# Transposing bf16 pairs as 32-bit words and using all 128 matmul columns for one matrix, in a batched matmul on one core

## The chip, the cores and the metric

One core of a Trainium2 chip. The metric is device time in microseconds (us), as the median of several executions of the same kernel.

## The reference

```python
# x [8, 16, 256, 512] fp32, weight [8, 16, 512, 384] fp32 -> out [8, 16, 256, 384] fp32
def reference(x, weight):
    return np.matmul(x, weight).astype(np.float32)
```

There are 128 independent products of a 256 x 512 matrix with a 512 x 384 matrix. Inputs and outputs together are 167.77 + 50.33 = 218.1 MB.

## The kernel before

The kernel goes through the batches two at a time ("a pair"). For a pair it loads 1 MB of x and two weights of 768 KB, casts both to bf16 on VectorE, transposes x on TensorE (16 tiles of 128 x 128), copies the transposed tiles from PSUM (the buffer into which TensorE's results go) on VectorE, multiplies, evacuates the products on ScalarE and stores 768 KB. All loads and stores are issued by SyncE.

```python
groups = [2] * ((B - GX) // 2) + [1] * GX     # GX = 2: 63 pairs, then two single batches
LAG = 4                                        # a store is issued four pairs late
...
def transpose_x(x_sb, RG):
    ...
    for r0 in range(0, R, 4):
        nc.vector.tensor_copy(out=x_bf[:, r0 : r0 + 4], in_=x_sb[:, r0 : r0 + 4])   # fp32 -> bf16
        for r in range(r0, r0 + 4, 2):
            pt = psum_t.tile([P, 2, KO, P], bf16, name="pt")
            for rr in range(2):
                for ko in range(KO):
                    nc.tensor.transpose(pt[:, rr, ko, :], x_bf[:, r + rr, ko::KO], identity)
            j = r % RG
            nc.vector.tensor_copy(out=x_t[:, j : j + 2, :, :, r // RG], in_=pt[:])
...
for n, G in enumerate(groups):
    ...                                        # C = 128 // G rows of each batch, RG row groups
    x_sb = load_x(b); w_sb = [load_w(b + i) for i in range(G)]
    x_t = transpose_x(x_sb, RG)
    w_bf = [...]                               # both weights cast to bf16
    if last:
        while waiting: store(nc.sync)
    for r in range(0, RG, 2):
        po = psum_o.tile([P, 2, 512], fp32, name="po")
        for rr in range(2):
            for ko in range(KO):
                for i in range(G):             # two batches side by side, 64 columns each
                    c0 = (b % GX + i) * CX
                    nc.tensor.matmul(po[i * C : (i + 1) * C, rr, :N],
                                     x_t[:, r + rr, ko, c0 : c0 + CX, :], w_bf[i][:, ko, :],
                                     start=(ko == 0), stop=(ko == KO - 1))
        nc.scalar.copy(out=out_sb[:, r : r + 2, :], in_=po[:, :, :N])
    waiting.append(...)
    if len(waiting) > LAG or last: store(nc.sync)
```

## Time and profile before

| | before |
|---|---|
| time, median of 3 executions | 526.35 us (526.27 to 526.38) |
| span of the profiled execution | 524.1 us |
| busiest compute engine | TensorE, 65% |
| DMA rate from 5 to 510 us | 423 GB/s |
| a pair of batches | 8.03 us |

The prediction below shows the lines that say what bounds this kernel. Four groups of instructions are what the change is about. A line names the source line, engine, operation, what is written and read with shapes, and the count; after the bar stand the total busy time in us and the mean duration of one in ns; after the second bar the idle time ahead of them and what ended most of it.

```profile
L125 PE MATMUL po<-w_bf,x_t 128*64 128x384 bf16 (+1 forms) x2032 | 271.0, 400 | 136.3 <-DVE w_bf L110 135.9
...
L132 ACT COPY out_sb<-po 128x768 f32<-128x768 f32 x128 | 102.5, 801 | 416.0 <-PE po L125 404.5
...
L86 DVE COPY x_t<-pt 128x1024 bf16<-128x1024 bf16 x128 | 83.6, 696 | 59.2 <-PE pt L82 59.2
L82 PE MATMUL pt<-identity,x_bf 128*128 128x128 bf16 x1024 | 70.3, 222 | 44.1 <-DVE x_bf L77 43.7
```

There are 2,032 matmuls of mostly 64 columns, 1,024 transposes, and 128 evacuating copies of all 128 partitions. ScalarE stands idle for 416 us; it has room for twice as many copies.

### The profile page before, as it was taken

The numbers are of one execution on the slowest core, as the hardware profiler recorded it, in microseconds if no ns is written. First come the engines' busy times: TensorE is split into PE (matmuls) and PEld (weight loads), VectorE is DVE, ScalarE is ACT, GpSimd is POOL, SyncE is SP. The second block draws the span as 40 slices with busy tenths as digits, with TensorE's granted clock in tenths as the row PEclk, the third lists the DMA queues.
The fourth block names the chain that finished last, engine by engine and source line by source line (L and its number), as shares of the span: only waits on it lengthen the run. The fifth ranks groups of instructions, "written<-read, shape, count | busy, mean of one in ns | idle before, by whom it ended". The sixth has DMA issues, their size and how long they took to land.

```text
span 524.1 us, 7422 instructions
## 1 busy us (share of the span) xinstructions
PE 339.3 (65%) x3056; PEld 231.8 (44%) x3056; DVE 273.4 (52%) x320; ACT 103.8 (20%) x129; POOL 0.7 (0%) x6
## 2 busy tenths in 40 slices
PE   4666758558576665675857657567666586556664
PEld 2444435345444443443534435444344354344442
DVE  4565464564554645546456455564554645645543
ACT  0222122121121121212212112212121121121221
POOL 0000000000000000000000000000000000000000
PEclk9989797986978889979798887988788879898888
DMA  8999999999999999999999999999999999999996
GB/s 347 418 413 423 422 424 420 424 424 419 426 420 423 423 419 425 422 424 422 424 424 423 421 425 423 425 422 423 425 423 424 423 424 425 423 422 425 423 425 272
DMA packets 37041, 218.59 MB, mean 417 GB/s; under 512 B 4112, under 2 KB 4112, under 8 KB 28816
## 3 DMA queue, kind: packets, MB, share of 16 engines
q1 hardware_dynamic: 37008, 218.12, 99.9%
q8 instruction: 24, 0.39, 0.3%
q14 instruction: 9, 0.07, 0.0%
HBM read 167.77 MB, written 50.33 MB: 416 GB/s over the span
## 4 chain that ended last, share of the span: by engine, by line
DMA 97%; PE 1%; DVE 1%; issue 0%; ACT 0%; SPq 0%; ACTq 0%; DVEq 0%
DMA x_sb<-in_x_dram 94%; DMA w_sb<-in_weight_dram 3%; PE po L125 1%; DVE x_t L86 0%; DVE x_bf L77 0%; DVE w_bf L110 0%; ACT out_sb L132 0%; PE pt L82 0%; SPq L60 0%; ACTq L132 0%; DVEq L77 0%
## 5 line engine op out<-in xcount | busy, mean ns | idle before, releaser
L125 PE MATMUL po<-w_bf,x_t 128*64 128x384 bf16 (+1 forms) x2032 | 271.0, 400 | 136.3 <-DVE w_bf L110 135.9
L125 PEld LDWEIGHTS <-x_t 128*64 128x64 bf16 (+1 forms) x2032 | 171.5, 132 | 219.8 <-DVE w_bf L110 122.8
L132 ACT COPY out_sb<-po 128x768 f32<-128x768 f32 x128 | 102.5, 801 | 416.0 <-PE po L125 404.5
L77 DVE CAST x_bf<-x_sb 128x2048 bf16<-128x2048 f32 x64 | 78.5, 1227 | 182.0 <-DMA x_sb<-in_x_dram 182.0
L110 DVE CAST w_bf<-w_sb 128x1536 bf16<-128x1536 f32 x128 | 116.7, 952 | 1.9 <-DMA w_sb<-in_weight_dram 1.9
L86 DVE COPY x_t<-pt 128x1024 bf16<-128x1024 bf16 x128 | 83.6, 696 | 59.2 <-PE pt L82 59.2
L82 PE MATMUL pt<-identity,x_bf 128*128 128x128 bf16 x1024 | 70.3, 222 | 44.1 <-DVE x_bf L77 43.7
L82 PEld LDWEIGHTS <-x_bf 128*128 128x128 bf16 x1024 | 60.3, 115 | 67.7 <-DVE x_bf L77 63.5
L132 ACT ACT_TABLE_LOAD x1 | 1.3, 1283 | 0.7 <-PEq L156 0.7
masks.py:199 POOL TENSOR_SCALAR_AFFINE_SELECT identity<-identity 128x128 bf16<-128x128 bf16 x1 | 0.3, 294 | 0.1
masks.py:197 POOL MEMSET identity<- 128x128 bf16 x1 | 0.2, 205 | 0.3 <-POOLq L156 0.3
L156 POOL MEMSET const-bfloat16-1.0<- 128x1 bf16 x1 | 0.1, 102 | 0.0
L156 POOL MEMSET const-uint8-127<- 128x1 uint8 x1 | 0.1, 102 | 0.0
L156 POOL MEMSET const-float32-0.0<- 128x1 f32 x1 | 0.1, 99 | 0.2 <-issue 0.2
L156 POOL MEMSET const-float32-1.0<- 128x1 f32 x1 | 0.1, 99 | 0.0
## 6 DMA issues: line engine op xcount, KB each, us to landing
w_sb<-in_weight_dram SPq DMA_DIRECT2D x128, 768.0 KB, 16.0
x_sb<-in_x_dram SPq DMA_DIRECT2D x64, 1024.0 KB, 16.0
out_dram<-out_sb SPq DMA_DIRECT2D x63, 768.0 KB, 16.0
out_dram<-out_sb SPq DMA_DIRECT2D x2, 384.0 KB, 3.0
```

The source lines that it names most:

```text
L77: nc.vector.tensor_copy(out=x_bf[:, r0 : r0 + 4], in_=x_sb[:, r0 : r0 + 4])
L82: nc.tensor.transpose(pt[:, rr, ko, :], x_bf[:, r + rr, ko::KO], identity)
L86: nc.vector.tensor_copy(out=x_t[:, j : j + 2, :, :, r // RG], in_=pt[:])
L110: nc.vector.tensor_copy(out=t[:], in_=w_sb[i][:])
L125: nc.tensor.matmul(po[i * C : (i + 1) * C, rr, :N], x_t[:, r + rr, ko, c0 : c0 + CX, :], w_bf[i][:, ko, :], start=(ko == 0), stop=(ko == K ...
L132: nc.scalar.copy(out=out_sb[:, r : r + 2, :], in_=po[:, :, :N])
L156: nc = _bacc.Bacc("TRN2", target_bir_lowering=False, num_devices=1)
```

## The change

The intent is fewer TensorE instructions. The transposes see two neighbouring bf16 values as one 32-bit word, so eight of them do the work of sixteen. A matmul takes its 128 columns from one batch instead of 64 from each of two, so sixteen do the work of thirty-two, and each weight is used up before the next one. The product's rows then do not lie on the partitions from which they are stored, so the evacuating copy moves 64 partitions at a time to where they belong: four copies per pair instead of two. At the end, each batch of the last pair is stored on its own, from 64 partitions.

```diff
-    identity = const.tile([P, P], bf16)
+    identity = const.tile([P, P], fp32)
...
-        x_t = xt_pool.tile([P, RG, KO, P, H], bf16, name="x_t")
+        x_t = xt_pool.tile([P, J, KO // 2, G, G, C, 2], bf16, name="x_t")
+        words = x_bf[:].bitcast(fp32)
...
-                pt = psum_t.tile([P, 2, KO, P], bf16, name="pt")
+                pt = psum_t.tile([P, 2, KO // 2, P], fp32, name="pt")
                 for rr in range(2):
-                    for ko in range(KO):
+                    for h in range(KO // 2):
                         nc.tensor.transpose(
-                            pt[:, rr, ko, :], x_bf[:, r + rr, ko::KO], identity
+                            pt[:, rr, h, :], words[:, r + rr, h :: KO // 2], identity
                         )
...
+        if last:
+            while waiting:
+                store()
+        x_t = transpose_x(x_sb)
+        out_sb = out_pool.tile([P, R, N], fp32, name="out_sb")
+        for i in range(G):
+            w_bf = wb_pool.tile([P, KO, N], bf16, name="w_bf")
+            nc.vector.tensor_copy(out=w_bf[:], in_=w_sb[i][:])
+            po = psum_o.tile([P, J, 512], fp32, name="po")
+            for j in range(J):
                 for ko in range(KO):
-                    for i in range(G):
-                        ... po[i * C : (i + 1) * C, rr, :N], x_t[:, r + rr, ko, c0 : c0 + CX, :] ...
+                    nc.tensor.matmul(
+                        po[:, j, :N],
+                        x_t[:, j, ko // 2, i, :, :, ko % 2].rearrange("k g c -> k (g c)"),
+                        w_bf[:, ko, :], start=(ko == 0), stop=(ko == KO - 1),
+                    )
-            nc.scalar.copy(out=out_sb[:, r : r + 2, :], in_=po[:, :, :N])
+            mine = slice(i * C, (i + 1) * C)
+            for g in range(G):
+                nc.scalar.copy(out=out_sb[mine, g::G, :], in_=po[g * C : (g + 1) * C, :, :N])
+            if last:
+                waiting.append((o_rows[(b + i) * M : (b + i + 1) * M].rearrange(
+                    "(p r) n -> p r n", r=R), out_sb[mine]))
+                store()
```

More of the change, by code (lines that the diff above doesn't have):

```diff
@@ L32 @@
     bf16 = mybir.dt.bfloat16
-    GX = 2
-    CX = P // GX
-    R = GX * M // P
-    groups = [2] * ((B - GX) // 2) + [1] * GX
+    G = 2
+    C = P // G
+    R = G * M // P
+    J = R // G
     LAG = 4
@@ L50 @@
     wb_pool = ctx.enter_context(tc.tile_pool(name="wb_pool", bufs=4))
-    out_pool = ctx.enter_context(tc.tile_pool(name="out_pool", bufs=LAG + 3))
+    out_pool = ctx.enter_context(tc.tile_pool(name="out_pool", bufs=7))
     psum_t = ctx.enter_context(tc.tile_pool(name="psum_t", bufs=2, space=bass.MemoryType.PSUM))
     psum_o = ctx.enter_context(tc.tile_pool(name="psum_o", bufs=3, space=bass.MemoryType.PSUM))
-    identity = const.tile([P, P], bf16)
+    identity = const.tile([P, P], fp32)
     make_identity(nc, identity)
@@ L60, in load_x @@
         nc.sync.dma_start(
-            x_sb[:], x_rows[b * M : (b + GX) * M].rearrange("(p r) k -> p r k", r=R)
+            x_sb[:], x_rows[b * M : (b + G) * M].rearrange("(p r) k -> p r k", r=R)
         )
@@ L68, in load_w, with transpose_x @@
         return w_sb
-    def transpose_x(x_sb, RG):
-        H = R // RG
+    def transpose_x(x_sb):
         x_bf = xb_pool.tile([P, R, K], bf16, name="x_bf")
-        x_t = xt_pool.tile([P, RG, KO, P, H], bf16, name="x_t")
+        x_t = xt_pool.tile([P, J, KO // 2, G, G, C, 2], bf16, name="x_t")
+        words = x_bf[:].bitcast(fp32)
         for r0 in range(0, R, 4):
@@ L78, in transpose_x @@
             for r in range(r0, r0 + 4, 2):
-                pt = psum_t.tile([P, 2, KO, P], bf16, name="pt")
+                pt = psum_t.tile([P, 2, KO // 2, P], fp32, name="pt")
                 for rr in range(2):
-                    for ko in range(KO):
+                    for h in range(KO // 2):
                         nc.tensor.transpose(
-                            pt[:, rr, ko, :], x_bf[:, r + rr, ko::KO], identity
+                            pt[:, rr, h, :], words[:, r + rr, h :: KO // 2], identity
                         )
-                j = r % RG
+                j, g = divmod(r, G)
                 nc.vector.tensor_copy(
-                    out=x_t[:, j : j + 2, :, :, r // RG], in_=pt[:]
+                    out=x_t[:, j, :, :, g : g + 2].rearrange(
+                        "k h i g c e -> k g (h i) (c e)"
+                    ),
+                    in_=pt[:].bitcast(bf16).rearrange(
+                        "k g h (i ce) -> k g (h i) ce", i=G
+                    ),
                 )
@@ L91, with store @@
     waiting = []
-    def store(queue):
+    def store():
         dram, out_sb = waiting.pop(0)
-        queue.dma_start(out=dram, in_=out_sb)
-    b = 0
-    for n, G in enumerate(groups):
-        last = n == len(groups) - 1
-        C = P // G
-        RG = G * M // P
-        if b % GX == 0:
-            x_sb = load_x(b)
-        w_sb = [load_w(b + i) for i in range(G)]
-        if b % GX == 0:
-            x_t = transpose_x(x_sb, RG)
-        w_bf = []
-        for i in range(G):
-            t = wb_pool.tile([P, KO, N], bf16, name="w_bf")
-            nc.vector.tensor_copy(out=t[:], in_=w_sb[i][:])
-            w_bf.append(t)
+        nc.sync.dma_start(out=dram, in_=out_sb)
@@ L112 @@
+    for b in range(0, B, G):
+        last = b == B - G
+        x_sb = load_x(b)
+        w_sb = [load_w(b + i) for i in range(G)]
         if last:
             while waiting:
-                store(nc.sync)
-        out_full = out_pool.tile([P, 2 * M // P, N], fp32, name="out_sb")
-        out_sb = out_full[:, :RG]
-        for r in range(0, RG, 2):
-            po = psum_o.tile([P, 2, 512], fp32, name="po")
-            for rr in range(2):
-                for ko in range(KO):
-                    for i in range(G):
-                        c0 = (b % GX + i) * CX
-                        nc.tensor.matmul(
-                            po[i * C : (i + 1) * C, rr, :N],
-                            x_t[:, r + rr, ko, c0 : c0 + CX, :],
-                            w_bf[i][:, ko, :],
-                            start=(ko == 0),
-                            stop=(ko == KO - 1),
-                        )
-            nc.scalar.copy(out=out_sb[:, r : r + 2, :], in_=po[:, :, :N])
@@ L133 @@
-        waiting.append(
-            (
-                o_rows[b * M : (b + G) * M].rearrange("(p r) n -> p r n", r=RG),
-                out_sb,
-            )
-        )
-        if len(waiting) > LAG or last:
-            store(nc.sync)
-        b += G
+                store()
[6 more added lines that the diff above has]
+            for j in range(J):
+                for ko in range(KO):
+                    nc.tensor.matmul(
+                        po[:, j, :N],
+                        x_t[:, j, ko // 2, i, :, :, ko % 2].rearrange("k g c -> k (g c)"),
+                        w_bf[:, ko, :],
+                        start=(ko == 0),
+                        stop=(ko == KO - 1),
+                    )
[6 more added lines that the diff above has]
+                store()
@@ L145 @@
+        if not last:
+            waiting.append(
+                (o_rows[b * M : (b + G) * M].rearrange("(p r) n -> p r n", r=R), out_sb[:])
+            )
+            if len(waiting) > LAG:
+                store()
 _INS = ['x', 'weight']
```

## The prediction

> **What bounds the kernel now.** I read the page first: the share each engine is busy, the slices, then the chain that ended last.
>
> ```profile
> PE 339.3 (65%) x3056; PEld 231.8 (44%) x3056; DVE 273.4 (52%) x320; ACT 103.8 (20%) x129; POOL 0.7 (0%) x6
> ...
> DMA  8999999999999999999999999999999999999996
> ...
> q1 hardware_dynamic: 37008, 218.12, 99.9%
> q8 instruction: 24, 0.39, 0.3%
> ...
> HBM read 167.77 MB, written 50.33 MB: 416 GB/s over the span
> ...
> DMA 97%; PE 1%; DVE 1%; issue 0%; ACT 0%; SPq 0%; ACTq 0%; DVEq 0%
> ```
>
> No compute engine is above 65%, while the sixteen DMA engines are full in every slice but the first and last, and the chain that ended last is DMA for 97%. The tensors are 167.77 + 50.33 = 218.1 MB, which both kernels must move. One pair of batches is (2 x 512 + 2 x 768 + 768) KB = 3.41 MB, and the casts of the input start every 8.03 us (493.86, 501.89, 509.93 in the timeline): 3.41 / 8.03 = 424 GB/s.
>
> Second, the waits of the DMA-issuing queue, to see whether an engine ever holds a transfer back:
>
> ```profile
> SPq L67 <- DMA w_sb<-in_weight_dram: 175.8, 118, 2.9
> SPq L60 <- DMA x_sb<-in_x_dram: 117.9, 58, 2.1
> SPq L95 <- DMA out_dram<-out_sb: 85.9, 57, 2.9
> SPq L95 <- ACT out_sb L132: 14.6, 4, 7.5
> ...
> SPq L67 <- DVE w_bf L110: 2.6, 2, 2.1
> SPq L67 <- DVE x_t L86: 2.3, 8, 0.4
> ```
>
> The issuer waits nearly always for an earlier transfer: in the instruction order each issue waits for the one eight before it. So eight are always in flight (16.0 us from issue to landing, about 8 x 1.9 us). VectorE held a load back for about 5 us in all, ScalarE a store for 14.6 us, all of that at the end. Compute has slack; only the two ends of the run can show it.
>
> Third, the end, in the timeline:
>
> ```profile
> 509.93 1.23 DVE L77 CAST x_bf<-x_sb 128x2048 bf16<-128x2048 f32 x1 [3.06 <-DMA x_sb<-in_x_dram]
> 511.21 0.93 PEld L82 LDWEIGHTS <-x_bf 128*128 128x128 bf16 x16 [1.91 <-DVE x_bf L77]
> ...
> 511.89 2.46 DVE L86 COPY x_t<-pt 128x1024 bf16<-128x1024 bf16 x2 [0.73 <-PE pt L82]
> 514.25 0.94 DVE L110 CAST w_bf<-w_sb 128x1536 bf16<-128x1536 f32 x1
> ...
> 515.25 4.45 PE L125 MATMUL po<-w_bf,x_t 128*128 128x384 bf16 x16 [2.95 <-DVE w_bf L110]
> 515.55 0.96 DVE L110 CAST w_bf<-w_sb 128x1536 bf16<-128x1536 f32 x1 [0.35 <-DMA w_sb<-in_weight_dram]
> ...
> 519.78 0.80 ACT L132 COPY out_sb<-po 128x768 f32<-128x768 f32 x1 [1.34 <-PE po L125]
> ```
>
> The last input lands at 509.9 and the last weight at 515.5; the final store leaves at 520.6 and lands at 523.0, 1.1 us before the span ends. The packet records show DMA work too: after 515 only about ten of sixteen engines are busy, and the latest still has packets of the queued stores at 521. From 509.9 that latest engine must move six 768 KB transfers (1.855 us each at 424 GB/s) and two of 384 KB (0.93 each): 509.9 + 11.1 + 1.9 = 522.9, which is when the last store lands. So even the end is nearly as tight on DMA as on compute.
>
> [...] TensorE has 6,114 rows in its order, 6,114 x 64 = 391 KB, and the instruction queue above moved 24 packets, 0.39 MB. [...]
>
> **The change part by part**, per pair of batches (budget 8.03 us).
>
> *Transposes, TensorE.* 16 bf16 transposes become 8 of 32-bit words. The 16 take 1.08 us for the run, 68 ns each. If a word goes at the same pace, 8 x 0.068 = 0.54 us[...]. I take about 1 us: no change.
>
> *Matmuls.* 32 of 64 columns become 16 of 128. The 32 take 0.51 + 2.76 us where the clock is full (504.12 to 507.75 in a mid-run window) because the two halves run side by side. Those of the last two batches already are 128 wide: 16 in 4.45 us at half clock, 0.28 each; full clock should give about 0.17, 16 x 0.17 = 2.7 us. No gain in time, half the instructions.
>
> *VectorE.* The copies of transposes still read 1,024 bf16 elements from PSUM and write runs of 128: 2 x 0.70 us as before. Casts unchanged. 4.3 us per pair stays; at worst, if the new pattern runs at half rate, 5.7 us.
>
> *ScalarE.* 2 copies of 128 x 768 become 4 of 64 x 768. The number of partitions should not shorten a copy (my assumption), so 256 x 0.80 = 205 us, 39% of the span, against 102.5; 3.2 us per pair.
>
> [...] All of it is beside the DMA: effect on the middle 0.
>
> *Instruction fetch.* This part does touch the bound engine. In the packet records one fetch of 16,384 bytes holds a DMA engine for 1.00 to 1.10 us, and the data packet after it typically takes about 0.64 instead of 0.234: some 1.4 us per fetch on one engine. Intervals of the input in the chain are 16.0 us but for two of 17.46 and 17.44 (starting at 185.96 and 364.10), just where fetches fall (190.8, 364.7): 1.45 us each, because a load is complete only when its slowest engine is. After has 2,305 TensorE rows, with hidden loads for 512 transposes some 2,800: 2,305 x 64 / 16,384 = 9 to 2,817 x 64 / 16,384 = 11 fetches instead of 24. Mean saving 13 or 14 x 1.4 / 16 = 1.2 us; on the slowest engine probably one hit less. I take -1.2 us.
>
> *The end.* Both weights are now issued ahead of the four waiting stores, so the last weight lands 1.86 us sooner. Two copies instead of one, +0.8 us, end ScalarE's part. The chain from the last input: cast 1.25, second weight landed by 3.8, x_t copies done by about 4.3, cast 0.95, 8 matmuls 1.4 to 2.6, two copies 1.6, so the last store leaves 8.2 to 10 us after the input against 10.7 before. But the latest DMA engine still has its 11.1 us of transfers, so this gain is mostly not cashed; it can close a gap of about 0.3 us. The last two stores change from 128 partitions x 3,072 bytes to 64 x 6,144. [...] Estimate +1.0 - 0.3 = +0.7 us.
>
> *Sum*: 526.35 + 0 (middle) - 1.2 (fetch) + 0.7 (end) = 525.85, told as 525.9 us.
>
> **Rivals.** (1) *TensorE becomes the bound.* [...] For it: the granted clock in before is 0.79 to 0.88 in many windows, and the matmuls at the end ran at 0.5. [...] I give it 4%. (2) *ScalarE, doubled, holds TensorE back through its three PSUM buffers.* 3.2 us in 8.03, each buffer freed 1.6 us after its last matmul, stores lagging four pairs: no effect, at most 0.8 us at the end. (3) *The half-partition stores cost their whole double time with nothing hidden*: +1.8 us, and with no fetch gain 528.2. (4) *The fetch saving counts in full on the slowest engine and the end gains*: two hits gone, -2.9, giving 523.5. (5) *The intended gain counts*: if half the instructions made the kernel faster by more than 2%, time would fall below 515.8; that needs 218.1 MB / 505 us = 432 GB/s averaged over the run, which no stage of the trace sustains.
>
> **Range and chances.** The small terms are each uncertain by about 1 us, and rival 3 stays inside; the low side is rival 4. So 525.9, range 523.8 to 528.8. Faster by over 2%: 0.01. Within: 0.95. Slower: 0.04, all of it rival 1.
>
> **What would show it.** Right: DMA still 97% of the chain and about 423 GB/s in the middle; the input's interval 16.0 us per two pairs; 9 to 12 packets in the instruction queue; ScalarE's busy time near 205 us with about 0.8 us per copy; TensorE matmuls per pair no faster. For the end: the last store's time from issue to landing, 2.4 us before[...]. Wrong: waits of the issuing queue put down to VectorE or ScalarE in the middle; word transposes above 0.3 us each; intervals above 8.1 us per pair; a mean DMA rate below 420.

The +1.0 in the end term supposed that a store from 64 partitions takes twice as long: 0.93 us more for the last one, little for the one before it. The kernel before has no such store, so its trace could not show this; the changed kernel's packets did later (468 ns against 234). Rival 3 rests on the same supposition. Half rate would have added to the 2.4 us from issue to landing (0.93, so 3.3). "About 1 us" for eight word transposes is the author's estimate; they took 1.20.

The hardware can be read from the traces, of before unless another is named. The 64 bytes per row: 24 packets of 16,384 bytes for 6,114 rows make 64.3. The halves side by side: two matmuls of 64 columns start 30 ns apart, and the next two 162 ns after the first two, so a full one was put at about 0.17 us. The clock: 1.00 was granted in the mid-run window (in the trace it is 304.12 to 307.75 us, not 504.12 to 507.75), and at the end 0.62 over the 4.45 us of the last matmuls, 0.50 from 516 to 519. That a load is complete only with its slowest engine: the last load of x has sixteen landings from 503.42 to 509.84 us, and its cast starts at 509.93. That the number of partitions does not shorten a copy was an assumption; the changed kernel took 794 ns for 64 partitions against 801 for 128.

## The result

The changed kernel took 526.51 us (median of 4, 526.10 to 526.97), the kernel before 526.37 us in the same rounds (4 executions, 526.27 to 526.95). The ratio is 1.0001, with a 95% interval of 0.9983 to 1.0018. A ratio here is the mean time of one kernel's fast runs over the mean of the other's fast runs of the same rounds, so it is not quite the ratio of the medians. The result is correct, and the time is the same.

The page of the changed kernel, in the lines that answer to those of before (busy time and instructions of each engine, DMA tenths, queues, chain, groups):

```profile
PE 324.2 (62%) x1536; PEld 187.1 (36%) x1536; DVE 272.8 (52%) x320; ACT 204.4 (39%) x257; POOL 0.7 (0%) x6
...
DMA  8999999999999999999999999999999999999997
...
q1 hardware_dynamic: 36880, 218.12, 100.2%
q8 instruction: 12, 0.20, 0.1%
...
HBM read 167.77 MB, written 50.33 MB: 416 GB/s over the span
...
DMA 97%; issue 1%; ACT 1%; SPq 0%; ACTq 0%
...
L126 ACT COPY out_sb<-po 64x768 f32<-64x768 f32 x256 | 203.2, 794 | 313.3 <-issue 274.1
L117 PE MATMUL po<-w_bf,x_t 128*128 128x384 bf16 x1024 | 232.5, 390 | 48.1 <-DVE x_t L85 38.1
...
L81 PE MATMUL pt<-identity,x_bf 128*128 128x128 f32 x512 | 92.2, 335 | 144.3 <-DVE x_bf L76 144.3
L85 DVE COPY x_t<-pt 128x1024 bf16<-128x1024 bf16 x128 | 82.7, 684 | 4.8 <-PE pt L81 4.8
```

The reader sees a kernel with half the TensorE instructions (3,056 to 1,536), twice the busy time on ScalarE (103.8 to 204.4 us) and the same DMA: full in every slice but the first and last, 97% of the chain, 416 GB/s over the span. The mean record of a matmul went only from 400 to 390 ns, although it now makes 128 columns instead of mostly 64: two halves side by side already overlapped. At a granted clock of 1.00, two of them started every 162 ns before (from 304.99 us on), and one full matmul starts every 163 ns after (from 310.56 us on). One full copy of 128 partitions took 801 ns, one of 64 takes 794: half the partitions save nothing. By the names on the page, queue q1 carries the data (218.12 MB), q8 and q14 carry instructions (0.20 and 0.08 MB). A packet is one record of the trace's DMA list, with a start, a duration and a size; those of 6,144 bytes mostly took 234 ns.

The middle, as one stretch of 160 us (start and end in us, length; then busy time and instructions of PE, PEld, DVE, ACT and POOL; then TensorE's granted clock, the busy share of the DMA engines, and GB/s), before:

```profile
200.00:360.00 160.00, 104.80 (x960) 71.93 (x957) 84.42 (x100) 32.02 (x40) 0.00 (x0) 0.87 1.01 423
```

and after:

```profile
200.00:360.00 160.00, 98.94 (x467) 57.26 (x466) 84.09 (x99) 62.26 (x79) 0.00 (x0) 0.84 1.01 423
```

All that changes is in columns that are not full. The last column, which sets the time, is 423 in both.

The waits of the queue that issues the DMAs, after (total us, times, longest us):

```profile
SPq L66 <- DMA w_sb<-in_weight_dram: 175.3, 119, 2.2
SPq L59 <- DMA x_sb<-in_x_dram: 120.8, 58, 2.9
SPq L99 <- DMA out_dram<-out_sb: 88.0, 58, 2.8
SPq L99 <- ACT out_sb L126: 11.9, 4, 5.5
SPq L66 <- DVE x_t L85: 10.9, 30, 0.4
```

The issuer still waits for earlier transfers. The wait for VectorE grew from 2.3 to 10.9 us, thirty times at most 0.4 us. With eight transfers queued (16.1 us from issue to landing on the page, against 524 / 257 = 2.04 us per transfer), that never emptied the engines: the rate in the middle stayed at 423 GB/s.

The end of the run after, in the timeline (start, length, instructions, in brackets the idle time before and what ended it):

```profile
510.21 1.23 DVE L76 CAST x_bf<-x_sb 128x2048 bf16<-128x2048 f32 x1 [3.17 <-DMA x_sb<-in_x_dram]
...
511.58 1.20 PE L81 MATMUL pt<-identity,x_bf 128*128 128x128 f32 x8 [2.34 <-DVE x_bf L76]
...
513.67 3.01 PE L117 MATMUL po<-w_bf,x_t 128*128 128x384 bf16 x16 [0.90 <-DVE x_t L85]
...
515.23 3.22 ACT L126 COPY out_sb<-po 64x768 f32<-64x768 f32 x4 [3.98 <-issue]
```

ScalarE is done at 518.45, where it was done at 520.58 before. The last store leaves at 518.48 instead of 520.6, 2.1 us sooner. The span ends at 524.2 instead of 524.1. So compute was done 2.1 us sooner, and the time did not show it. Why not is what the experiments had to find.

**Where the end went.** The trace has sixteen landings for each transfer (4,112 for 257), read here as one per DMA engine. The sixteen of one load lie up to 6.4 us apart at about 500 us, and what waits for the load starts after the last of them: the last load of x landed from 503.42 to 509.84 us before and its cast started at 509.93; after, it landed from 503.89 to 510.11, fifteen of the sixteen by 508.49, and the cast started at 510.21. Worked out from these landing records (us from the span's start; the last transfer of each kernel, and the lag of the slowest engine behind the fastest at about 500 us):

```
                     last store   first     15th      16th     first-to-last
                     issued       engine    engine    engine   lag at 500 us
before               520.6        522.76    522.93    522.98   6.4
after                518.5        521.57    521.96    523.19   6.2
```

Before, fourteen engines had run empty by 521.0, but two, equally far behind, had packets of the store before until about 521.5, just when the first packets of the last store began (521.45). All sixteen then landed it within 0.2 us. So the end of the kernel before was held by compute and by its two slowest engines at once, as the prediction had worked out (522.9). After, fifteen engines finish at 521.96, a full microsecond sooner than before, and then one engine, 1.2 us behind them, ends the kernel where it had ended before. The 2.1 us of compute were not there to be won: the slowest DMA engine alone holds the end now.

**Where the instruction fetches went.** The fetches did halve, 24 packets to 12. They are packets of 16,384 bytes, 24 for the 6,114 TensorE rows before and 12 for 3,205 after, so 255 and 267 rows to a packet, and each took 1.00 to 1.10 us. What they cost the data that moves at the same time is the question here. Summing the data packets up to a given time gives the lead of the changed kernel in bytes moved, told in us at 424 GB/s:

```
us from start                   10     200     500     510     slowest engine has the last x at
before                           0       0       0       0     509.84
after                        -0.10    0.05    0.32    0.31     510.11
after, a second run          -0.09    0.23    0.47    0.46     509.91
```

The gain over the run is 0.32 + 0.10 = 0.42 us, in the second run 0.47 + 0.09 = 0.56, about what the saved bytes take: 12 x 16,384 B / 424 GB/s = 0.46 us. The slowest engine has none of it: it gets the last x 0.27 us later than before, and in the second run 0.07 us later. The average lag behind the fastest engine at 500 us fell from 56.7 / 16 = 3.5 us to 43.7 / 16 = 2.7 us, but the largest lag stayed (6.4 and 6.2 us). The intervals of the loads in the chain (of x before, of the weights after) say the same. After the first 42 us, two of them clearly exceed 16.0 us before, by 1.46 and 1.44, 2.9 in all. After, four do, by 0.67, 0.32, 0.79 and 0.74, 2.5 in all. The first 42 us have long ones too, 16.21 and 19.07 before, 16.79 and 17.52 after; the prediction's reading, "16.0 us but for two", had left out the one of 19.07.

The landing records also show which fetches these were. Where a 16,384-byte packet of q8 can be told apart, one engine's lag jumps by 1.45 to 1.6 us (before, at 22.6, 43.0, 236.3, 256.7, 364.7 and 431.2 us), and in five of these six it is an engine that was not among the slowest until then. But three of the four late intervals of the changed kernel contain no such packet. They contain packets of 8,192 bytes of q14, at 209.5, 339.1 and 468.6 us, and at each of these one engine's lag jumps by 0.7 to 0.8 us; at the first this makes it the slowest, and at the other two it is the slowest engine that is hit. (The second run shows the last two again, 0.76 and 0.78.) q14 grew from 10 such packets to 26 when 2,048 instructions were added on GpSimd (pool_nops_few, below), and the change, which halves TensorE's instructions, does not shorten it: 9 such packets before, 10 after (the page's 11 counts one of 32 bytes). Between these jumps the largest lag grows slowly, from 2.9 us at 223 to 3.7 at 336. So the two large hits on the slowest engine are gone, and smaller ones, by fetches that the change does not touch, stand in their place.

### The profile page after: what moved, and what is told of

The parts are those of the page before. It is cut to its first block, busy times and chain, and to the rows that moved or that the text cites. A ratio compares the mean times of both kernels' runs of the same rounds, so it can differ in the third digit from the quotient of the medians.

```text
span 524.2 us, 4635 instructions
## 1 busy us (share of the span) xinstructions
PE 324.2 (62%) x1536; PEld 187.1 (36%) x1536; DVE 272.8 (52%) x320; ACT 204.4 (39%) x257; POOL 0.7 (0%) x6
## 3 DMA queue, kind: packets, MB, share of 16 engines
q1 hardware_dynamic: 36880, 218.12, 100.2%
## 4 chain that ended last, share of the span: by engine, by line
DMA 97%; issue 1%; ACT 1%; SPq 0%; ACTq 0%
DMA w_sb<-in_weight_dram 94%; DMA x_sb<-in_x_dram 3%; ACT out_sb L126 1%; ACTq L162 0%; SPq L66 0%; SPq L59 0%
## 5 line engine op out<-in xcount | busy, mean ns | idle before, releaser
L126 ACT COPY out_sb<-po 64x768 f32<-64x768 f32 x256 | 203.2, 794 | 313.3 <-issue 274.1
L117 PE MATMUL po<-w_bf,x_t 128*128 128x384 bf16 x1024 | 232.5, 390 | 48.1 <-DVE x_t L85 38.1
L81 PE MATMUL pt<-identity,x_bf 128*128 128x128 f32 x512 | 92.2, 335 | 144.3 <-DVE x_bf L76 144.3
L117 PEld LDWEIGHTS <-x_t 128*128 128x128 bf16 x1024 | 109.7, 114 | 163.2 <-DVE x_t L85 60.1
L113 DVE CAST w_bf<-w_sb 128x1536 bf16<-128x1536 f32 x128 | 121.9, 955 | 38.6 <-DMA w_sb<-in_weight_dram 38.6
L81 PEld LDWEIGHTS pt<-identity,x_bf 128*128 128x128 f32 x512 | 77.4, 213 | 166.0 <-issue 164.9
## 6 DMA issues: line engine op xcount, KB each, us to landing
w_sb<-in_weight_dram SPq DMA_DIRECT2D x128, 768.0 KB, 16.1
x_sb<-in_x_dram SPq DMA_DIRECT2D x64, 1024.0 KB, 16.1
out_dram<-out_sb SPq DMA_DIRECT2D x63, 768.0 KB, 16.1
```

Of the source, the lines that this page charges most:

```text
L81: nc.tensor.transpose(pt[:, rr, h, :], words[:, r + rr, h :: KO // 2], identity)
L113: nc.vector.tensor_copy(out=w_bf[:], in_=w_sb[i][:])
L117: nc.tensor.matmul(po[:, j, :N], x_t[:, j, ko // 2, i, :, :, ko % 2].rearrange("k g c -> k (g c)"), w_bf[:, ko, :], start=(ko == 0), stop= ...
L126: nc.scalar.copy(out=out_sb[mine, g::G, :], in_=po[g * C : (g + 1) * C, :, :N])
```

## The experiments

Two theories stood against each other for the end. *Half rate*: the two stores from 64 partitions take double time and eat the gain. *Slowest engine*: one of sixteen DMA engines lags, and a sooner last store cannot end the kernel before that engine has worked off its queue. For the middle: *DMA only*, against a hidden cost of compute.

### one_store: the last pair stored whole

```diff
-            if last:
-                waiting.append((... one batch ..., out_sb[mine])); store()
-        if not last:
-            waiting.append((... the pair ..., out_sb[:]))
-            if len(waiting) > LAG: store()
+        waiting.append((... the pair ..., out_sb[:]))
+        if last or len(waiting) > LAG: store()
```

> The changed kernel, but the last pair of batches leaves in one store over all 128 partitions (768 KB) after both batches, instead of two stores of 64 partitions. Theory (half-partition stores run at half rate: in the changed kernel their 6,144-byte packets took 468 ns against 234): packets of the last store at 234 ns again, issue near 518.4 us as now, packets over by about 521.2 us, last landing about 1 us earlier; time 525.5 against 526.5 of the changed kernel. Rival (the end is set by when ScalarE delivers the last half, the transfer's rate does not matter): the last store is twice as large and can't start earlier, so no gain or up to 0.9 us slower, 526.5 to 527.4.

Measured: 526.25 us (526.11 to 526.28, 5 executions), before 526.42 (11 executions), ratio 0.9997 (0.9985 to 1.0009). Correct. In the changed kernel, while most engines work on the last two stores, most of the packets (6,144 bytes each) take about 468 ns instead of 234, so these do run at half rate. Here they take 234 to 259. But the time did not move: the store leaves at 518.51, fifteen engines have landed it by 521.77, the slowest by 523.22. Half rate is real and does not set the end. The changed kernel's own packets show why: from 521.33 us on, only the slowest engine has packets left, and these take 234 ns each although they are of a half-partition store. This run alone is not clean, since the whole pair in one store is twice the bytes at twice the rate: 768 KB at 424 GB/s takes 1.86 us, as long as the last half-store takes at half rate. It was also the warning that landing 3.3 us after issue does not show half rate: here it is 3.26 with full-rate packets.

### row_stores and row_stores_apart: two small stores over all partitions

To have the last store both small and over 128 partitions, the last pair's matmuls are ordered so that half the rows of both batches are done first.

```diff
+        if last:
+            for i, j in [(0, 0), (0, 1), (1, 0), (1, 1)]:
+                # row_stores:       po is one of two tiles, one per batch i, made ahead of the loop
+                # row_stores_apart: po = psum_o.tile(...) here, one per (i, j)
+                ... four matmuls, two copies of 64x384 to out_sb[i*C:(i+1)*C, j*G+g, :] ...
+                if i == G - 1:
+                    rows = slice(j * G, (j + 1) * G)
+                    nc.sync.dma_start(out=dram[:, rows, :], in_=out_sb[:, rows, :])
```

> The changed kernel, but the last pair is finished row block by row block, so its two stores (384 KB each) each cover all 128 partitions with 3,072 bytes a partition. Theory of the half-rate stores: packets of 3,072 bytes at about 122 ns as in the kernel before, each store 0.95 us of transfer instead of 1.9; last issue near 518.4 us, landing about 520.8 us, so 2 us less than the changed kernel: 524.5, and 1.8 us less than the kernel before. Rival (the lag of the slowest DMA engine and the compute chain set the end): within 0.5 us of 526.4.

Measured: 526.84 us (526.04 to 528.18, 6 executions, three near 526.2 and three from 527.4 up, the profiled one among these), ratio 1.0009 (0.9993 to 1.0024). Correct, and inconclusive through a slip of mine: two halves shared a PSUM tile, so the matmuls of one waited for ScalarE's copies of the other. The timeline shows it in the brackets:

```profile
516.42 2.40 PE L136 MATMUL po<-w_bf,x_t 128*128 128x384 bf16 x7 [0.48 <-ACT out_sb L144]
...
519.88 1.44 PE L136 MATMUL po<-w_bf,x_t 128*128 128x384 bf16 x4 [1.06 <-ACT out_sb L144]
```

The last store left only at about 522.3. The second version gives each half its own tile.

> The row-block stores again, with a PSUM buffer of its own for every block, so that no matmul waits for a copy of another block (in the first try TensorE waited 0.5 and 1.1 us for that and the last store left at 522.3). Last issue near 518.3 us. Theory of the half-rate stores: last landing near 520.8 us on all engines, time 524.5. Theory of the slowest DMA engine (one of sixteen is 1.6 us behind the others and has its bytes to move whatever the stores look like; it ended at 523.19 in the changed kernel and at 523.22 with one store): fifteen engines land by about 521.2 us, the last one at about 523.2 us, time within 0.4 us of 526.4.

Measured: 526.22 us (525.84 to 526.50, 5 executions), before 526.45 (9 executions), ratio 0.9997 (0.9985 to 1.0010). Correct. The store's timeline:

```profile
517.52 1.31 SPq L150 DMA_DIRECT2D out_dram<-out_sb  x2
```

Both stores go out from 517.52 on, the second at about 518.5, with packets of 3,072 bytes at 121 to 124 ns, so at full rate. Fifteen engines land the last one by 521.43, 0.5 us sooner than in the changed kernel. The slowest lands it at 523.25, where it landed before. This is the clean test: full rate, small and early, and the end has not moved. It was also meant as the version that beats both kernels, and it does not: its interval contains 1.

### dma_only: the DMA alone

Transposes, casts, matmuls and copies are taken out; loads and stores stay, and the stores send a tile that was zeroed once. Its output is wrong, which doesn't matter for the time.

```diff
+    const_out = const.tile([P, R, N], fp32); nc.vector.memset(const_out[:], 0.0)
...
-        x_t = transpose_x(x_sb)
-        out_sb = out_pool.tile([P, R, N], fp32, name="out_sb")
+        out_sb = const_out
-            ... casts, matmuls, copies ...
```

> All loads and stores of the changed kernel in the same order and sizes, no compute at all, stores from a constant tile: wrong result on purpose. Theory (compute is hidden; it shows only at the end): the middle keeps 423 to 424 GB/s and the time falls only by what the end waits for compute, 1.5 to 3 us: about 524. Rival (compute or its waits hold transfers back in the middle): rate above 427 GB/s in the middle and a time below 520.

Measured: 523.41 us (522.88 to 523.99, 4 executions), ratio 0.9944 (0.9931 to 0.9957).

```profile
q14 instruction: 2, 0.02, 0.0%
HBM read 167.77 MB, written 50.33 MB: 418 GB/s over the span
```

Without any compute the kernel is 3.0 us shorter than before (526.42 - 523.41). That is all that any change to compute could win, the fetching of its instructions included: the only fetches left are two packets of 8 KB. Over the run, this kernel gains 0.93 us in bytes (its lead goes from -0.04 at 20 us to 0.89 at 500), and its slowest engine has the last x at 508.39, 1.45 us sooner than before. It has even so one engine that is 1.6 us behind the fifteenth (last landing 521.35 against 519.72) and 3.0 behind the first. The largest lag jumps by 0.6 us at each of the two fetches, at 146 and 404 us.

### compute_before, compute_after, compute_bf16: compute alone

Here the DMA is taken out instead: x and the weights of one pair are loaded once, and only the last store is issued. Their outputs are wrong, which doesn't matter for the times. The three differ in compute alone: the kernel before, the changed kernel, and the changed kernel with its word transposes undone (sixteen bf16 transposes, but matmuls of 128 columns and shifting copies).

```diff
-        x_sb = load_x(b)
-        w_sb = [load_w(b + i) for i in range(G)]
+        if b == 0:
+            x_once = load_x(b); w_once = [load_w(b + i) for i in range(G)]
+        x_sb, w_sb = x_once, w_once
-        ... all stores but the last ...
# compute_bf16 also:
-    identity = const.tile([P, P], fp32)
+    identity = const.tile([P, P], bf16)
-                    for h in range(KO // 2): transpose(pt[:, rr, h, :], words[:, r + rr, h :: KO // 2], identity)
+                    for ko in range(KO): transpose(pt[:, rr, ko, :], x_bf[:, r + rr, ko::KO], identity)
```

> The kernel before without its DMA: one pair of inputs loaded once and used 64 times, only the last group stored; wrong result on purpose. It shows what the compute of before takes when nothing hides it. VectorE alone needs 4.34 us per pair (280 us); the loop matmuls 2.8 to 3.3, transposes 1.1, last copy 0.7, both weight casts 1.8, handovers 0.3 gives 6.7 to 7.2 us per pair. Expected 300 to 460 us, below the 526 of the whole kernel. If compute were near the bound, it would be above 500.

> The changed kernel without its DMA in the same way; wrong result on purpose. Theory (the change does shorten TensorE's part, the DMA hides it): a first matmul waits for one weight cast instead of two, loop 0.95 + 2.9 + 1.2 + 0.7 + 0.3 = 6.0 us per pair, so 5 to 15% below the compute of before. Rival (nothing to gain even without DMA, as half columns side by side already went at the rate of full columns and word transposes take 150 ns each): within 3% of the compute of before; VectorE at 4.2 us per pair is the floor of both, 270 us.

> One part alone, without DMA: the changed kernel's full-column matmuls and shifted ScalarE copies, but 16 bf16 transposes per pair as in the kernel before instead of 8 word transposes; wrong result on purpose. If the word transposes give the gain: slower than the changed kernel's compute by 8 x (0.150 x 0 to 0.07) = up to 0.5 us per pair, 30 us. If they give nothing (8 took 1.20 us in the changed kernel, 16 took 1.08 in the kernel before): same within 10 us, or faster.

| | time, median of 4 | ratio to the kernel before, 95% |
|---|---|---|
| compute_before | 303.86 us | 0.5767 (0.5755 to 0.5779) |
| compute_after | 277.59 us | 0.5274 (0.5267 to 0.5281) |
| compute_bf16 | 278.12 us | 0.5290 (0.5277 to 0.5302) |

As compute, the change is good: 277.59 / 303.86 = 0.914, 8.6% shorter, at a granted clock of 0.99 to 1.00 in all three (the whole kernels have 0.84 to 0.88). Nearly all of it comes from the matmuls, their order and their copies; undoing the word transposes costs 0.5 us of 278, and the two intervals overlap. My reason for the gain, as it was expected, was at best half right. I had put it on a loop through TensorE of 6 to 7 us per pair, in which the first matmul waits for one cast weight instead of two; a pair takes about 4.7 us in compute_before and 4.3 in compute_after. The stretch from 100 to 200 us of compute_before shows VectorE nearly full instead, and what it waits for (total us, times, longest us):

```profile
100.00:200.00 100.00, 85.48 (x1078) 59.58 (x1078) 93.82 (x115) 35.40 (x45) 0.00 (x0) 1.00 0.01 2
```

```profile
DVE w_bf L111 <- PE po L126: 16.6, 59, 0.3
```

and of compute_after:

```profile
100.00:200.00 100.00, 91.64 (x592) 62.21 (x591) 100.00 (x124) 77.71 (x99) 0.00 (x0) 1.00 0.00 1
```

VectorE went from 93.8% to 100%. In compute_before, its cast of the weights waited 59 times for the matmuls to free a buffer: with two batches side by side, both weights are in use to the end of the pair. In the new order each is free as soon as its own batch is done, and the wait is gone. The chains that ended last, first of compute_before, then of compute_after, agree that the matmuls had been part of the limit and VectorE alone is now:

```profile
PE 60%; DVE 19%; issue 17%; DMA 2%; DVEq 0%; ACT 0%; ACTq 0%
```

```profile
DVE 91%; issue 3%; DMA 2%; PE 2%; ACT 1%; ACTq 0%
```

No run changed the number of weight buffers alone, so that the buffers are the reason is read from the waits and not tested.

The difference of the spans is 301.8 - 275.7 = 26.1 us. VectorE's part makes it up: 16.6 of this wait, 267.2 - 260.6 = 6.6 less busy time, and 3.6 - 1.0 = 2.6 less waiting for transposes, 25.8 together. In the real kernel a pair has 8.03 us and none of this is seen. With the DMA in place, these 26 us of compute were worth nothing.

### pool_nops, pool_nops_few, after_again: what does instruction fetch cost?

These add instructions that do nothing, on GpSimd, which is otherwise idle, so that only the fetch of them is new.

```diff
         w_sb = [load_w(b + i) for i in range(G)]
+        for _ in range(75):        # pool_nops_few: 32;   after_again: no edit
+            tc.keep_in_program_order(nc.gpsimd.engine_nop())
```

> The changed kernel with 4,800 empty instructions on GpSimd, which computes nothing here: 4,800 x 64 bytes = 307 KB more instruction fetch, some 37 packets of 8 KB, and nothing else. Theory of bytes (a fetch costs the DMA engines its bytes at 424 GB/s): 0.7 us more, DMA progress behind the changed kernel by 0.7 us at the end of the fetches. The prediction's theory (a fetch costs the time its packet took plus the delay of the next): 37 x (0.31 + 0.35) / 16 = 1.5 us more. If fetch does not matter: 0.

Measured: 545.89 us (median of 4 executions, one of them slow; ratio of the fast ones 1.0366, 1.0350 to 1.0382). Correct, and it answered nothing. The fast runs, 545.1 to 546.4 us, come to 0.114 us for each of 4,800 empty instructions, so GpSimd had probably become the bound itself; I argue this from the time alone. The profiled execution was the slow one, at 752.34 us, with TensorE busy for 97% and no sign in the kernel of why. No reading is taken from it.

> The fetch question again with 2,048 empty GpSimd instructions, so that GpSimd is done in about 230 us (4,800 took 544 us, which is why the first try was bound by GpSimd and answered nothing): 131 KB, 16 more packets of 8 KB. Theory of bytes plus one engine: the bytes moved by all engines fall behind the changed kernel by 131 KB / 424 GB/s = 0.31 us at 300 us and stay there; the engine that is hit falls behind the others by 1.0 us per hit. If the hits are spread over sixteen engines, the slowest ends about 1 us later and the time is 527.0 to 527.8; if they go to one engine, it ends up to 16 us later, 540. The prediction's sum (time of the packet plus the delay of the next, over sixteen engines) would be 16 x 0.66 / 16 = 0.7 us behind in bytes.

> The changed kernel itself once more, for a narrower interval and a second look at its end. The same within 0.3%: 526.2 to 526.8. If one DMA engine again ends 1 us or more after the fifteen others, at about 523.2 us, the end is set by the slowest engine and not by chance of one run.

Measured: pool_nops_few 530.73 us (530.21 to 531.03, 4 executions), ratio to the kernel before 1.0080 (1.0064 to 1.0096); after_again, the changed kernel once more, 526.27 (525.86 to 526.67, 4 executions), ratio 0.9998 (0.9984 to 1.0012). Both correct. So 2,048 empty instructions, 131 KB, cost about 4.5 us (530.73 - 526.27). The queue lines of instructions, first the q14 line of the changed kernel (its q8 line stands above), then those of pool_nops_few:

```profile
q14 instruction: 11, 0.08, 0.0%
```

```profile
q8 instruction: 12, 0.20, 0.1%
q14 instruction: 26, 0.21, 0.1%
HBM read 167.77 MB, written 50.33 MB: 412 GB/s over the span
```

Sixteen more packets of 8 KB came in (26 against 10, without the one of 32 bytes), all in the first 81 us, one in about 5 us. In bytes they are little: 131 KB / 424 GB/s = 0.31 us. From 80 us on the kernel is 0.43 to 0.62 us behind the changed one in data moved, between the 0.31 of the bytes alone and the 0.7 that the prediction's way of counting gives, so this run does not decide between those two. Either is far from 4.5 us. The landings show the rest (lag of each engine behind the fastest of the same transfer, in us, sorted):

```
after,         at  71 us:  0.0 0.0 0.2 0.2 0.2 0.2 0.3 0.4 0.4 0.6 0.6 1.0 1.0 1.0 1.1  1.5
pool_nops_few, at  69 us:  0.0 0.1 0.1 0.1 0.3 0.9 0.9 0.9 0.9 1.0 1.0 1.0 1.1 1.3 1.8 10.3
pool_nops_few, at 499 us:  0.0 0.4 0.4 0.7 1.0 2.3 2.4 2.5 2.6 2.9 3.1 3.8 3.8 3.9 5.9 10.5
```

The records do not name the engine of a packet, but only one engine falls so far behind, by 10.3 us in 70 us, and each of the first four packets adds 0.65 to 0.7 us to its lag, so the added packets must have hit that one. It stays that far behind to the end (10.5 us at 499): its share did not go to the fifteen others. Its lag at 500 us is 4.3 us larger than in the changed kernel (10.5 against 6.2), and the time is 4.5 us longer. The last load of x is complete when it has it, at 514.70 where the others have it by 510.15, and compute and the last store, landed at 527.85, follow from there. So one engine set the time here, and what these fetches cost depended on the engine that they hit, and not on their bytes alone.

## Why the prediction was right, and where a step failed

The time, 526.5 us, lies in the range and 0.66 above the 525.85 of the sum. What carried the prediction is its largest claim, that the middle does not change; that the small terms came out near is luck, as shown below. Point by point:

**The middle: right.** 423 GB/s before and after, DMA 97% of the chain, casts of the last three inputs at 494.08, 502.15 and 510.21 (8.065 us per pair). dma_only shows the reason in one number: all compute and the fetching of its instructions together cost 3.0 us of 526. Two of the signs named as "wrong" did turn up without an effect on the rate: the issuer's waits for VectorE (10.9 us in pieces of up to 0.4), and "word transposes above 0.3 us each": the mean record is 335 ns. As records overlap, this sign told little; eight take 1.20 us.

**Transposes, matmuls, copies: right within their width.** Eight word transposes took 1.20 us at a granted clock of 1.00 (1.70 at 0.63, 1.95 at 0.50), so 150 ns each, against the estimate of 1; sixteen bf16 ones took 1.08 at 1.00, 68 ns each. Sixteen matmuls took 3.01 us at 1.00, against 2.7, and 4.46 at 0.62. ScalarE's copies took 203.2 us, 794 ns each, against 205 and 800. None sat near a bound. The rival with TensorE as the bound did not come. The argument against it is cut, as the kernel before did not show it: its granted clock is 0.79 at 60 to 68 and 400 to 408 us and 1.00 at 200 to 208 with the same work per pair. What these runs show is that in the compute-only runs of the two kernels, where TensorE was busy for 82% and 87%, 0.99 to 1.00 was granted.

**Instruction fetch: the step that failed.** "I take -1.2 us", from 13 or 14 fetches less by 1.4 us over 16 engines. Twelve fetches fewer came (the trace has 3,205 TensorE rows, not 2,305 to 2,817). The packet records show 0.42 to 0.56 us for all engines together, about the bytes alone; the mean lag of an engine fell by 0.8 us; and the time, which follows the slowest engine, got none of it. The 1.4 us per fetch on its engine were read rightly (1.45 to 1.6 in the landings); the error was to average over the engines and to take it that "on the slowest engine probably one hit less" would be worth as much. The excess intervals after 42 us added up to 2.9 us before, two hits of the size of a TensorE fetch, and to 2.5 after: three hits by 8 KB packets of q14, which the prediction had not counted, and one in an interval that holds a packet of each queue (106 to 123 us).

**The end: the size was near, the mechanism was not.** "+1.0 - 0.3 = +0.7 us". The half-partition stores did take double time while most engines worked on them: 468 ns for a 6,144-byte packet against 234. But one_store and row_stores_apart, which have none, end at the same time. The term of +1.0 was therefore wrong. The compute part of the step was right: the last store left 8.3 us after the input's cast began (518.48 - 510.21), predicted 8.2 to 10, against 10.7 before. The end is held by the slowest engine, which the prediction had named for the kernel before (its 522.9 by summing queued transfers) and then added a second cost to. The time from issue to landing, for which it had set 2.4 us as a sign, or 3.3 at half rate, was 4.7 on the slowest engine (523.19 - 518.48) and 3.5 on fifteen; one_store with full-rate packets gives 4.7 and 3.26. That sign told nothing apart.

**The sum.** With -1.2 replaced by 0 and +0.7 by about +0.2 (523.19 - 522.98), the working gives about 526.55, and 526.51 came. Both replacements are read from the result, so this is bookkeeping and no second prediction; the difference is within what these runs can tell apart (the interval of the ratio is 0.9 us wide to each side). Two wrong terms of opposite sign had partly cancelled. That is luck, and the time alone would not have shown it.

**What stays open.** The records carry no engine number, so which of the sixteen engines lags, and why these fetches fall on it, cannot be read. A part of the lag in the full kernels also grows at times when no fetch is near (around 32 us in the kernel before, slowly from 223 to 336 us in the changed one). The slow execution of pool_nops was not explained.

## What to carry to other kernels

Where DMA is full, find first what the kernel takes with compute removed: here 523.4 of 526.4 us, so that an 8.6% better compute loop was worth nothing. Read the landings of single DMA engines, not only their mean load: here the cast of the last x waited for the last of sixteen landings, 6.2 us after the first, and a saving of 0.42 us over all engines did not reach the slowest, which had the last x 0.27 us later. Look at the instruction stream as DMA traffic too: TensorE's was 0.39 MB before and 0.20 after, and 2,048 empty instructions, 0.31 us by their bytes, cost about 4.5 us when one engine fell 10.3 us behind.
